# RWKV scan: even heads in one half of the partitions and odd heads in the other, all products 64x64x64

## Chip, core and metric

The kernel runs on one core of one Trainium2 chip. The metric is the device time of one execution in microseconds (us). Three runs of the kernel before gave a median of 3237.41 us (3236.87 to 3237.65).

## What is computed

The program is one transformer block: two modulated layer norms, a token mixer with two branches (neighbourhood attention and an RWKV recurrence), a merge of the branches, and an expert layer. The change touches the recurrence, which runs in both directions (d = 0, 1) over 256 context tokens and then 1024 tokens, for 8 heads of 64:

```
def step(S, inp):
    r_t, w_t, k_t, a_t, v_t, kk_t = inp
    sa = einsum('bhvk,bhk->bhv', S, -kk_t)
    S = S * w_t[:, :, None, :] + sa[..., None] * (kk_t * a_t)[:, :, None, :] + v_t[..., None] * k_t[:, :, None, :]
    y = einsum('bhvk,bhk->bhv', S, r_t)
S, ys = lax.scan(step, S0, xs, reverse=reverse)
```

## The kernel before, in words

The recurrence is computed in chunks of 64 tokens: 20 chunks for each direction, 4 of context and 16 of the sequence. Inside a chunk it is a set of matrix products, so that a chunk and a direction make one step, and one step takes the state S of each head from one chunk's end to the next. The program has these parts in order of time:

- **Projections and features** (the function `mixer`, up to about 898 us of the trace). `proj` multiplies the normalised tokens by the input weights (L256). `feat` makes, for four pairs of heads (`ct` 0 to 3; a pair is two heads of 64 in 128 partitions) and both directions, the operands of every chunk and stores them to DRAM scratch: X (L417), the masked products AQ (L424 to L431), the transposed BK (`BTD`, L439), the token-major values v (`vD`, L361). `inv_load`, `inv` and `inv_off` invert the 64x64 triangles of all chunks on VectorE and store them as `WD`.
- **The scan** (`rwkv_chain`, L513 to L570). A step loads its operands with 7 DMAs on the SP queue, two buffers for each direction: X, AQ in two pieces, BT, WT in two pieces, and v into the lower half of the tile UV. Its products: RY from X and the block-diagonal S (L536, 4 products of 128x128x128) and from AQ and UV (L539, 8 of 128 rows by 64 columns); R = -RY copied by ScalarE and VectorE, one half each (L543, L544); US = WT R (L548, 8 products of 64x64x64); the result copied into the upper half of UV by VectorE and ScalarE (L551); BT UV (L554, 8 products); the state update, an addition and a multiplication for each half (L559, L560, four VectorE instructions); and, after the context, the output's second part (L563, 8 products), a copy on ScalarE (L566) and a store on the ScalarE queue (L567). GpSimd clears the unused quarters of AQ and UV in each step (L527).
- **Attention** (`attention`) runs over four head pairs with 8 blocks each. A block computes scores (L586 to L589), a row maximum with the bias (L590, L591), an exponential on ScalarE (L594), a normalisation (L597), transposes with their copies (L604 to L608), and the output (L611 to L615). The preparation of Q and K of a head pair is in L621 to L641, loads of bias (`bt`, one buffer, L650) and values (`vb`, L655) go out on the ScalarE queue. The pairs 0 and 1 have one PSUM buffer for each kind of tile; the pairs 2 and 3 have two.
- **Readout** (`readout`, L661 to L693) sums both directions' outputs, needs the scan's end, and is followed by modulation chunks (L117) and the two branch products (L707). The expert layer fills the rest from about 1600 us.

A tile framework orders the instructions of each engine when the program is built, by its own estimates and by the order in which the program is written; at run time each engine takes its list in that order. So the place of the attention blocks among the scan's steps is fixed in the program, and can be read from it.

Of the kernel before, what the change touches and what calls it, by code (L numbers as in the profile page):

```python
# [63 lines left out]
def host_layout(i):  # L64

    f=np.float32
# [82 lines left out]
def mixer(octx, tc, i, G, keep, mc, dbg=None):  # L149
# [14 lines left out]
    vnD=dp.tile([TS,512],F32,name="vnD"); vD=dp.tile([TS,512],F32,name="vD")  # L164
    DLD=[dp.tile([4,128,20],F32,name=f"DLD{d}") for d in range(2)]
    XD=[dp.tile([4,128,20,128],F32,name=f"XD{d}") for d in range(2)]
    AQD=[dp.tile([20,128,8,128],F32,name=f"AQD{d}") for d in range(2)]
    BTD=[dp.tile([20,128,4,128],F32,name=f"BTD{d}") for d in range(2)]
    WD=[dp.tile([4,40,64,64],F32,name=f"WD{d}") for d in range(2)]
    aD=[dp.tile([4,2,40,64,32],F32,name=f"aD{d}") for d in range(2)]; sgD=dp.tile([128,T],F32,name="sgD")  # L170
    G.update(dict(XD=XD,AQD=AQD,BTD=BTD,WD=WD,DLD=DLD))
    gD=dp.tile([16,128,T],F32,name="gD")
    yD=[dp.tile([T,512],F32,name=f"yD{d}") for d in range(2)]
# [5 lines left out]
    with ExitStack() as c1:  # L179
# [142 lines left out]
        with ExitStack() as c3:  # L322
# [29 lines left out]
            def on_v(c,ps):  # L352
                ct=(c-2560)//128
                for q,(t0,nt) in enumerate(((0,2),(2,4),(6,4))):
# [6 lines left out]
                    nc.sync.dma_start(vD[t0*128:(t0+nt)*128,ct*128:(ct+1)*128].rearrange("(a p) f -> p a f",p=128),vt[:,:nt])  # L361
# [5 lines left out]
            def feat(ct,mid):  # L367
# [18 lines left out]
                for d in range(2):  # L386
# [21 lines left out]
                    for jb in range(5):  # L408
# [33 lines left out]
                    bo=bonus[:,:,2*ct:2*ct+2]; pv=pt[:,:16].rearrange("p (a b) -> p a b",b=2)  # L442
# [70 lines left out]
def rwkv_chain(p,pR,tc,i,G):  # L513
    nc=tc.nc; vD=G["vD"]; yD=G["yD"]
    S=[p.tile([128,4,2,64],F32,name=f"S{d}",bufs=1) for d in range(2)]
    for d in range(2): nc.gpsimd.memset(S[d],0.0)
    DL=[p.tile([128,4,20],F32,name=f"DLs{d}",bufs=1) for d in range(2)]
    for d in range(2): nc.sync.dma_start(DL[d],G["DLD"][d].rearrange("a p c -> p a c"))
    def step(j,n,d):
        main=j>0; tb=tblock(j,d); c=n if d==0 else 3-n; cc=tb*4+c  # L520
        first=(j==0 and n==0); M=128 if main else 64
        X=p.tile([128,4,128],F32,name=f"cX{d}"); AQ=p.tile([128,8,128],F32,name=f"cAQ{d}")
        BT=p.tile([128,4,128],F32,name=f"cBT{d}"); WT=p.tile([128,4,64],F32,name=f"cWT{d}")
        UV=p.tile([128,512],F32,name=f"UV{d}")
        nc.sync.dma_start(X[:,:,:M],G["XD"][d][:,:,cc,:M].rearrange("a p f -> p a f"))
        nc.sync.dma_start(AQ[64:128,:,:M],G["AQD"][d][cc][64:128,:,:M])
        nc.gpsimd.memset(AQ[0:64,:,0:64],0.0); nc.gpsimd.memset(UV[0:64],0.0)  # L527
        if main: nc.sync.dma_start(AQ[0:64,:,64:128],G["AQD"][d][cc][0:64,:,64:128])
        nc.sync.dma_start(BT,G["BTD"][d][cc])
        for hh in range(2):  # L530
            nc.sync.dma_start(WT[hh*64:hh*64+64],G["WD"][d][:,cc*2+hh,0:64,:].rearrange("a s t -> s a t"))
        nc.sync.dma_start(UV[64:128],vD[cc*64:(cc+1)*64,:])
        RY=pR.tile([128,512],F32,name=f"RY{d}")
        if not first:
            for ct in range(4):
                nc.tensor.matmul(RY[:M,ct*128:(ct+1)*128],X[:,ct,:M],S[d][:,ct].rearrange("p a b -> p (a b)"),  # L536
                    start=(ct==0),stop=False,skip_group_check=True)
        for hd in range(8):
            nc.tensor.matmul(RY[0:64,hd*64:(hd+1)*64],AQ[:,hd,0:64],UV[:,hd*64:(hd+1)*64],  # L539
                start=(first and hd==0),stop=True,skip_group_check=True)  # L540
        R=p.tile([128,4,64],F32,name=f"R{d}",bufs=2)
        ry=RY[0:64].rearrange("p (a b f) -> p a b f",a=4,b=2)
        nc.scalar.activation(R[0:64],ry[:,:,0,:],AF.Copy,scale=-1.0)  # L543
        nc.vector.tensor_scalar_mul(R[64:128],ry[:,:,1,:],-1.0)  # L544
        US=pR.tile([128,512],F32,name=f"US{d}")
        for hd in range(8):
            ct,hh=divmod(hd,2); h=slice(hh*64,hh*64+64)
            nc.tensor.matmul(US[h,ct*64:(ct+1)*64],WT[h,ct,:],R[h,ct,:],start=True,stop=True)  # L548
        uv=UV[0:64].rearrange("p (a b f) -> p a b f",a=4,b=2); us=US[:,0:256].rearrange("p (a f) -> p a f",a=4)
        for hh in range(2):  # L550
            (nc.scalar.copy if hh else nc.vector.tensor_copy)(uv[:,:,hh,:],us[hh*64:hh*64+64])  # L551
        for hd in range(8):
            ct,hh=divmod(hd,2)
            nc.tensor.matmul(US[hh*64:hh*64+64,256+ct*64:256+(ct+1)*64],BT[:,ct,hh*64:hh*64+64],  # L554
                UV[:,hd*64:(hd+1)*64],start=True,stop=True)
        sp=US[:,256:512].rearrange("p (a b) -> p a b",b=64)
        for hh in range(2):
            h=slice(hh*64,hh*64+64); sd=S[d][h,:,hh,:]
            if not first: nc.vector.tensor_add(sd,sd,sp[h])  # L559
            nc.vector.tensor_tensor(sd,sp[h] if first else sd,DL[d][h,:,cc:cc+1].to_broadcast([64,4,64]),op=ALU.mult)  # L560
# [538 lines left out]
```

## Time and profile before

| | us |
|---|---|
| median of three runs | 3237.41 |
| the profiled execution | 3229.26 |
| its span, first to last instruction | 3227.5 |
| TensorE busy, share of the span | 2969.2, 92% |
| VectorE busy | 2357.7, 73% |
| ScalarE busy | 1740.9, 54% |
| GpSimd busy | 640.3, 20% |
| mean granted TensorE clock | 0.958 of full speed |

The profile is of one execution. TensorE's busy time counts a product from its start to its modelled end, so overlapping products make a busy share that is near one long before the array is full. A float32 product shows as two records. Times of day below (898, 1225, ...) are us from the span's start. All further rows stand in the section on rows.

### The profile page before, as it was taken

What the parts mean: (1) busy time and instruction counts of PE and PEld (TensorE: products, weight loads), DVE (VectorE), ACT (ScalarE), POOL (GpSimd) and SP (SyncE); (2) the same over time, 40 slices, a digit from 0 to 9 for tenths busy, and PEclk for the clock granted to TensorE, in tenths of its full rate; (3) what the DMA queues carried; (4) which work ended last, traced back from release to release, by engine and by line L of the source; (5) the groups of instructions that cost most, each with busy time, mean ns of one, the idle gap of its engine ahead of it and who ended that gap; (6) DMA issues with size and microseconds to landing.
All of it is one profiled execution on the core that took longest, in us unless ns stands there. A gap on an engine that the chain in (4) does not pass through costs nothing.

```text
span 3227.5 us, 47411 instructions
## 1 busy us (share of the span) xinstructions
PE 2969.2 (92%) x17900; PEld 2361.8 (73%) x17900; DVE 2357.7 (73%) x3207; ACT 1740.9 (54%) x2006; POOL 640.3 (20%) x511
## 2 busy tenths in 40 slices
PE   5999999998779879999879999999999999999996
PEld 3777777776667765577668888888888878888884
DVE  3335555443566768857779899888888888888887
ACT  4343333333234343432357777777777777777775
POOL 2233333333331326411000000111010111010004
PEclk9999999998789989999889999999999999999998
DMA  5245444455768776544589999999999999999985
GB/s 192 82 125 136 120 117 120 125 139 146 165 175 196 188 184 215 157 158 150 191 317 383 387 372 370 358 360 378 381 362 364 355 365 376 381 362 363 363 319 230
DMA packets 537640, 825.17 MB, mean 256 GB/s; under 512 B 206590, under 2 KB 335742, under 8 KB 537284
## 3 DMA queue, kind: packets, MB, share of 16 engines
q1 hardware_dynamic: 489436, 742.36, 67.3%
q10 hardware_dynamic: 42616, 60.26, 5.9%
q0 software_dynamic: 5360, 19.54, 2.3%
q8 instruction: 141, 2.31, 0.3%
q14 instruction: 87, 0.71, 0.1%
HBM read 732.49 MB, written 89.55 MB: 255 GB/s over the span
## 4 chain that ended last, share of the span: by engine, by line
PE 56%; DVE 14%; DMA 10%; issue 6%; ACT 3%; SPq 2%; POOL 1%; ACTq 0%; POOLq 0%; DVEq 0%
PE ph L1014 21%; PE ye L1029 14%; PE pp L256 7%; DVE lo L913 4%; PE pA L707 3%; PE po L750 2%; DVE tmp L290 1%; DVE W L293 1%; DMA raw<-in_w_e_dram 1%; PE px L424 1%; PE pt L1051 1%; DMA AU<-aD 1%; ACT hi L912 1%; DMA bt<-in_bias_dram 1%; DMA vb<-vnD 1%
## 5 line engine op out<-in xcount | busy, mean ns | idle before, releaser
L913 DVE TENSOR_TENSOR lo<-raw,hi 128x2048 fp32r<-128x2048 f32 (+1 forms) x560 | 1197.4, 2170 | 108.7 <-ACT hi L912 92.6
L912 ACT CAST hi<-raw 128x2048 fp32r<-128x2048 f32 (+1 forms) x560 | 1010.0, 1814 | 355.3 <-PE ph L1014 191.9
L1014 PE MATMUL ph<-lo,xh 128*128 128x512 f32 (+1 forms) x1536 | 456.8, 379 | 23.6 <-DVE lo L913 21.9
L1014 PE MATMUL ph<-hi,xh 128*128 128x512 f32 (+1 forms) x1536 | 449.2, 374 | 3.1 <-ACT xh L884 2.0
L1014 PE MATMUL ph<-hi,xl 128*128 128x512 f32 (+1 forms) x1536 | 448.2, 373 | 0.0
L1014 PEld LDWEIGHTS ph<-lo,xh 128*128 128x128 f32 x1536 | 267.8, 189 | 95.7 <-DVE lo L913 48.4
L1014 PEld LDWEIGHTS ph<-hi,xh 128*128 128x128 f32 x1536 | 271.5, 188 | 55.9 <-ACT xh L884 2.4
L1014 PEld LDWEIGHTS ph<-hi,xl 128*128 128x128 f32 x1536 | 270.9, 188 | 52.5
L256 PE MATMUL pp<-uh,whi 128*128 128x512 f32 (+1 forms) x832 | 263.8, 390 | 4.7 <-DVE th L332 3.1
L256 PE MATMUL pp<-ul,whi 128*128 128x512 f32 (+1 forms) x832 | 266.9, 390 | 0.1
L256 PE MATMUL pp<-uh,wlo 128*128 128x512 f32 (+1 forms) x832 | 261.9, 387 | 1.0 <-issue 0.7
L862 POOL DMA_INDIRECT gath<-table,idx x16 | 37.8, 2364 | 959.2 <-DVE oh L854 587.8
L1029 PE MATMUL ye<-lo,dh 128*128 128x512 f32 x704 | 222.8, 398 | 1.1 <-DVE lo L913 1.1
L1029 PE MATMUL ye<-hi,dh 128*128 128x512 f32 x704 | 219.8, 393 | 2.5 <-ACT hi L912 1.3
L1029 PE MATMUL ye<-hi,dl 128*128 128x512 f32 x704 | 218.9, 392 | 3.1 <-DVE dl L1053 3.1
L256 PEld LDWEIGHTS pp<-uh,wlo 128*128 128x128 f32 x832 | 155.9, 195 | 39.2 <-issue 9.4
L256 PEld LDWEIGHTS pp<-uh,whi 128*128 128x128 f32 x832 | 154.4, 195 | 40.4 <-issue 6.8
L256 PEld LDWEIGHTS pp<-ul,whi 128*128 128x128 f32 x832 | 155.7, 195 | 37.6 <-issue 9.4
L290 DVE TENSOR_TENSOR tmp<-AU,W 120x144 f32<-120x144 f32 (+24 forms) x248 | 88.4, 357 | 116.9 <-DMA WD<-AU 40.8
L1029 PEld LDWEIGHTS ye<-hi,dl 128*128 128x128 f32 x704 | 132.9, 189 | 32.1 <-DVE dl L1053 3.6
L244 POOL TENSOR_TENSOR wlo<-wraw,whi 128x512 fp32r<-128x512 f32 x86 | 113.6, 1339 | 209.4 <-ACT whi L243 141.0
L1029 PEld LDWEIGHTS ye<-hi,dh 128*128 128x128 f32 x704 | 131.2, 189 | 30.7 <-ACT hi L912 2.0
(334 smaller groups left out, 4470.2 us busy)
## 6 DMA issues: line engine op xcount, KB each, us to landing
raw<-in_w_e_dram SPq DMA_DIRECT2D x430, 1024.0 KB
raw<-in_w_e_dram SPq DMA_DIRECT2D x128, 768.0 KB
wraw<-in_w_in_dram SPq DMA_DIRECT2D x86, 256.0 KB
wmod<-in_w_mod_dram SPq DMA_DIRECT2D x48, 256.0 KB
BTD<-BT SPq DMA_DIRECT2D x40, 256.0 KB
cBT<-BTD SPq DMA_DIRECT2D x40, 256.0 KB
wmod<-in_w_mod_dram SPq DMA_DIRECT2D x16, 512.0 KB
XD<-X SPq DMA_DIRECT2D x32, 256.0 KB
```

The lines of the kernel that those rows point to most:

```text
L244: nc.gpsimd.tensor_sub(l[:,ks],r,h[:,ks].bitcast(F32))
L256: nc.tensor.matmul(p,wt[:,k,:],ut[:,k,a:a+b],start=(k==0 and first),stop=(k==7 and last))
L290: nc.vector.tensor_tensor(v,AU[d][:,:,s,ts_][:,:,None,:].to_broadcast([120,2,nj,L]), W[d][:,:,js,s:s+1].to_broadcast([120,2,nj,L]),op=ALU. ...
L293: for o,v in tv: nc.vector.tensor_sub(o,o,v)
L424: for c in range(4): nc.tensor.matmul(pa[:,c,:w],BK[h,c,:],X[h,c,:w],start=True,stop=True)
L707: nc.tensor.matmul(pq[q],w[:,kk,:],y[:,kk,q*512:(q+1)*512],start=(kk==0 and first),stop=(kk==3 and last))
L750: nc.tensor.matmul(pq[q],a[:,r],w[:,q*512:(q+1)*512],start=(k==0 and first),stop=(k==7 and last))
L862: gi=nc.gpsimd.indirect_dma_start(out=g,out_offset=None,in_=table[:,:], in_offset=bass.IndirectOffsetOnAxis(ap=idx[:,:1],axis=0))
L912: nc.scalar.copy(hi[:,:2*w],r[:,:2*w])
L913: li=nc.vector.tensor_sub(lo[:,:2*w],r[:,:2*w],hi[:,:2*w].bitcast(F32))
L1014: nc.tensor.matmul(PH[m][j][:,:c.stop-c.start],x[:,k,:],y[:,c],start=(k==0 and a),stop=(k==7 and b))
L1029: nc.tensor.matmul(ye[j],l[:,k,:],rr[:,j*512:(j+1)*512],start=st and a,stop=sp and b)
```

## The change

Before, an operand of one head could lie in any half of the partitions: AQ held the part for v in partitions 64 to 127 and the part for the corrections in 0 to 63, and both heads of a pair stood side by side in the columns. After the change every operand of an even head lies in partitions 0 to 63 and every operand of an odd head in 64 to 127: AQ becomes AV (for v) and AU (for the corrections U), UV becomes V and U, BT becomes two planes of 64 columns, S loses its zero blocks. Each product of 128 rows becomes two of 64 rows that add up in PSUM, and each is a 64x64x64 product on the diagonal of the array: a step has 64 products where it had 36. The parts that need only loaded data (AV V, BT V) or the old state (X S) stand ahead of the ones that need U. R and U are copied by one ScalarE instruction each over 128 partitions, the state update is two VectorE instructions, the output's copy covers 128 partitions by 256. The clearing by GpSimd is gone. A step has 8 loads (AV, two for V, X, two for WT, BT, AU) and two output stores. The features are stored in this layout: four stores for BTD where there was one, four for AVD and AUD where there were three, two for vD where there was one. The host permutes the columns of g_up, gn and w_pr accordingly.

```
-                        if jb: nc.sync.dma_start(AQD[d][cs,64:128,2*ct:2*ct+2,:]...,AQ[64:128])
                         for hh in range(2):
-                            if jb: nc.sync.dma_start(AQD[d][cs,0:64,2*ct+hh,64:128]...,AQ[0:64,:,hh,64:128])
-                            else: nc.sync.dma_start(AQD[d][cs,64:128,2*ct+hh,:w]...,AQ[64:128,:,hh,:w])
+                            nc.sync.dma_start(AVD[d][cs,hh*64:hh*64+64,ct,:w]...,AQ[64:128,:,hh,:w])
+                            if jb: nc.sync.dma_start(AUD[d][cs,hh*64:hh*64+64,ct]...,AQ[0:64,:,hh,64:128])
...
-                        nc.sync.dma_start(BTD[d][cs,:,ct,:].rearrange("c p f -> p c f"),BT)
+                        for j in range(2):
+                            for hh in range(2):
+                                nc.sync.dma_start(BTD[d][cs,j,hh*64:hh*64+64,ct]...,BT[j*64:j*64+64,:,hh*64:hh*64+64])
...
 def rwkv_chain(p,pR,tc,i,G):
+    H=[slice(0,64),slice(64,128)]
+    def mm(o,l,r,first=None,stop=False):
+        for ct in range(4):
+            for hh,h in enumerate(H):
+                b=first is not None and len(first)<2
+                z=nc.tensor.matmul(o[h,ct],l[h,ct],r[h,ct],start=b,stop=stop,skip_group_check=True)
...
+        nc.sync.dma_start(AV[:,:,:M],G["AVD"][d][cc][:,:,:M])
+        for h,hh in zip(H,range(2)): nc.sync.dma_start(V[h],vD[cc*64:(cc+1)*64,hh])
         nc.sync.dma_start(X[:,:,:M],G["XD"][d][:,:,cc,:M].rearrange("a p f -> p a f"))
...
+        nc.sync.dma_start(BT,G["BTD"][d][cc].rearrange("j p a k -> p j a k"))
+        if main: nc.sync.dma_start(AU,G["AUD"][d][cc])
+        mm(RU[:,0],AV[:,:,0:64],V,[],first)
+        if not first: mm(RU[:,0],X[:,:,0:64],S[d],stop=True)
         R=p.tile([128,4,64],F32,name=f"R{d}",bufs=2)
+        nc.scalar.activation(R,RU[:,0],AF.Copy,scale=-1.0)
+        f=[]
+        mm(YS[:,1],BT[:,1],V,f)
         if main:
+            mm(YS[:,0],AV[:,:,64:128],V,f)
+            mm(YS[:,0],X[:,:,64:128],S[d])
+        mm(RU[:,1],WT,R,stop=True)
+        nc.scalar.copy(U,RU[:,1])
+        mm(YS[:,1],BT[:,0],U,stop=True)
+        if not first: nc.vector.tensor_add(S[d],S[d],YS[:,1])
+        nc.vector.tensor_tensor(S[d],YS[:,1] if first else S[d],DL[d][:,:,cc:cc+1].to_broadcast([128,4,64]),op=ALU.mult)
+        if main:
+            mm(YS[:,0],AU,U,stop=True)
+            Y=p.tile([128,4,64],F32,name="Y",bufs=4)
+            nc.scalar.copy(Y,YS[:,0])
+            for h,hh in zip(H,range(2)): nc.scalar.dma_start(yD[d][(cc-4)*64:(cc-3)*64,hh],Y[h])
```

The order that the framework makes moves with it. On TensorE, in the middle of the scan before, the steps of both directions (RY and US) stand among attention's scores (sc, sl), transposes (apt) and outputs (yp); x8 is eight products of a kind, and the numbers tell tiles apart:

```order
L536 MATMUL RY_8487<-S_7293,cX_8473 128x128 x4
L539 MATMUL RY_8487<-UV_8477,cAQ_8474 64x64 x8
L536 MATMUL RY_8551<-S_7294,cX_8537 128x128 x4
L539 MATMUL RY_8551<-UV_8541,cAQ_8538 64x64 x8
L604 MATMUL apt<-ident,s 128x128
L586 MATMUL sc<-KH_10834,Q_10832 128x256
L587 MATMUL sc<-KL_10836,Q_10832 128x256
L588 MATMUL sl<-KH_10834,Q_10832 128x320
L589 MATMUL sl<-KL_10836,Q_10832 128x320
L548 MATMUL US_8503<-R_8500,cWT_8476 64x64 x8
L548 MATMUL US_8567<-R_8564,cWT_8540 64x64
L611 MATMUL yp<-pT,vc 64x128 x4
```

In the changed program the same engine has, from the first step after the context to the last one, nothing but the scan (all its products have the line of the helper, L533). One step of one direction against the other, in the middle:

```order
L533 MATMUL RU_8850<-R_8868,cWT_8838 64x64 x8
L533 MATMUL RU_8940<-cV_8929,cAV_8926 64x64 x8
L533 MATMUL RU_8940<-S_7460,cX_8925 64x64 x7
L533 MATMUL YS_8851<-U_8840,cBT_8841 64x64 x8
L533 MATMUL RU_8940<-S_7460,cX_8925 64x64
L533 MATMUL YS_8941<-cV_8929,cBT_8931 64x64 x8
L533 MATMUL YS_8941<-cV_8929,cAV_8926 64x64 x7
L533 MATMUL YS_8851<-U_8840,cAU_8837 64x64 x8
L533 MATMUL YS_8941<-cV_8929,cAV_8926 64x64
L533 MATMUL YS_8941<-S_7460,cX_8925 64x64 x8
```

All but one or two of the 16 attention blocks that stood among the scan's steps have moved behind the scan's last step: before, 16 blocks' outputs stand in ScalarE's list between the scan's first and last instruction, and after, none. The 8 blocks of the first head pair now stand among the 8 readouts, then 16 blocks follow with no other work between them, and the last 8 stand among the branch products, as 8 did before.

On ScalarE, a step's copies before stand among attention's casts, copies and loads:

```order
L543 ACTIVATE R_8500<-RY_8487 64x256
L625 DMA qz<-kD 128x512
L543 ACTIVATE R_8564<-RY_8551 64x256
L640 CAST Q_10832<-qz 64x2x128 x2
L640 CAST Q_10833<-qz 64x2x128 x2
L644 DMA vc<-vnD 128x2x128
L606 COPY pT<-apt 120x512
L551 COPY UV_8477<-US_8503 64x4x64
```

After, both directions' copies and stores alternate alone:

```order
L553 ACTIVATE R_10218<-RU_10200 128x256
L567 COPY Y<-YS_10111 128x256
L568 DMA yD_95<-Y 64x256 x2
L560 COPY U_10190<-RU_10200 128x256
L553 ACTIVATE R_10308<-RU_10290 128x256
L567 COPY Y<-YS_10201 128x256
L568 DMA yD_96<-Y 64x256 x2
L560 COPY U_10280<-RU_10290 128x256
```

The exponentials of the first attention block stand ahead of the first R after the context in this list, and those of the second block behind the scan's last U.

## Rows read from the trace of the kernel before

**Rows 1.** Table by stretch: scan, readout with attention, branch products with attention.

```profile
core 0: us, PE busy (x) PEld busy (x) DVE busy (x) ACT busy (x) POOL busy (x), PEclk, DMA share, GB/s
898.00:1225.00 327.00, 267.63 (x3416) 225.86 (x3414) 226.62 (x548) 125.87 (x295) 91.05 (x114) 0.91 0.77 184
1225.00:1350.00 125.00, 111.40 (x595) 55.40 (x595) 110.21 (x241) 55.28 (x123) 80.57 (x61) 0.95 0.67 210
1350.00:1466.00 116.00, 114.99 (x650) 91.71 (x648) 67.71 (x135) 36.57 (x72) 20.49 (x7) 1.00 0.44 139
```

**Rows 2.** One line's instructions: L614 in those three stretches, L566 and L594 over the span.

```profile
L614 ACT CAST yh<-yp x16: 247/265/267, 966.4 to 1198.2; 128x128 fp32r<-128x128 f32 x16
L614 ACT CAST yh<-yp x9: 241/265/273, 1240.0 to 1349.2; 128x128 fp32r<-128x128 f32 x9
L614 ACT CAST yh<-yp x7: 265/265/267, 1359.6 to 1421.0; 128x128 fp32r<-128x128 f32 x7
L566 ACT COPY Y<-RY x32: 580/580/582, 969.9 to 1223.8; 64x512 f32<-64x512 f32 x32
L594 ACT ACTIVATE s<-s,m x64: 758/820/880, 951.3 to 1408.9; 128x576 f32<-128x576 f32 x32, 128x696 f32<-128x696 f32 x32
```

**Rows 3.** Chain of waits in the scan's stretch, two of its longest pieces: start, us, what.

```profile
999.67 8.73 DMA bt<-in_bias_dram
...
1113.51 8.16 DMA vb<-vnD
```

**Rows 4.** Timeline of TensorE, scan products: start, us, engine, line, tiles, form, records.

```profile
1216.91 1.13 PE L536 MATMUL RY<-S,cX 128*128 128x128 f32 x8 [0.98 <-ACT R L543]
1217.97 1.15 PE L539 MATMUL RY<-UV,cAQ 128*64 128x64 f32 x16
...
1067.39 0.68 PE L548 MATMUL US<-R,cWT 64*64 64x64 f32 x16 [1.67 <-DVE R L544]
...
1069.80 1.11 PE L548 MATMUL US<-R,cWT 64*64 64x64 f32 x14
```

**Rows 5.** One line's instructions: loads issued on the SP queue (ns min/median/max).

```profile
L531 SPq DMA_DIRECT2D cWT<-WD x80: 573/593/892, 886.4 to 1207.5; - x80
L532 SPq DMA_DIRECT2D UV<-vD x40: 445/468/707, 846.2 to 1212.5; - x40
L668 SPq DMA_DIRECT2D y<-yD x16: 319/326/437, 1221.6 to 1295.6; - x16
```

**Rows 6.** DMA traffic of 900 to 1220 us in 40 slices: GB/s.

```profile
GB/s 281 211 125 207 117 244 221 165 110 200 192 217 224 205 181 184 211 188 156 233 165 154 259 103 234 189 192 194 200 213 193 169 172 191 225 172 124 204 158 54
```

**Rows 7.** VectorE groups by line and form, 898 to 1466 us: busy us, mean ns | idle before.

```profile
L560 DVE TENSOR_TENSOR S<-S,DLs 64x256 f32<-64x256 f32 x76 | 43.5, 572 | 1.9
L559 DVE TENSOR_TENSOR S<-S,US 64x256 f32<-64x256 f32 x76 | 31.7, 418 | 20.2 <-PE US L554 18.1 <-ACT UV L551 0.5
...
L591 DVE CUSTOM_DVE_ANT_0 s<-sl,bt,m 128x320 f32<-128x320 f32 x32 | 17.5, 548 | 17.9 <-DMA bt<-in_bias_dram 17.2
...
L544 DVE TENSOR_SCALAR R<-RY 64x256 f32<-64x256 f32 x40 | 16.6, 418 | 24.7 <-ACT R L543 23.6
L551 DVE COPY UV<-US 64x256 f32<-64x256 f32 x40 | 16.5, 414 | 13.3 <-PE US L548 11.3 <-issue 1.4
```

**Rows 8.** Features: what the BT copy (L438) waited for, its store, the stretch.

```profile
  DMA BTD<-BT: 12.9, 8
...
L439 SPq DMA_DIRECT2D BTD<-BT x40: 359/562/1249, 191.6 to 827.3; - x40
...
190.00:830.00 640.00, 589.69 (x3859) 461.93 (x3859) 329.62 (x697) 240.19 (x402) 236.49 (x179) 0.93 0.52 131
```

**Rows 9.** Table by stretch, as rows 1: the granted clock is the third value from the end.

```profile
919.00:936.00 17.00, 7.84 (x75) 7.15 (x76) 12.04 (x23) 3.30 (x9) 7.32 (x7) 0.50 0.56 150
950.00:1038.00 88.00, 81.29 (x1081) 67.88 (x1080) 58.46 (x165) 37.46 (x89) 17.51 (x29) 1.00 0.80 191
1069.10:1072.50 3.40, 3.40 (x30) 2.73 (x29) 3.21 (x10) 0.99 (x3) 0.47 (x1) 0.51 0.64 163
```

More of the change, by code (lines that the diff above doesn't have):

```diff
@@ L438, in feat @@
                         nc.scalar.copy(BT,pb.rearrange("p (c f) -> p c f",c=4))
[L439 removed]
+                        for j in range(2):
+                            for hh in range(2):
+                                nc.sync.dma_start(BTD[d][cs,j,hh*64:hh*64+64,ct].rearrange("c p f -> p c f"),BT[j*64:j*64+64,:,hh*64:hh*64+64])
                     pt=px.tile([128,512],F32,name="px")
                     for t in range(8): nc.tensor.matmul(pt[:,2*t:2*t+2],a[:,256+t*128:256+(t+1)*128],hsr[:,ct,2*ct:2*ct+2],start=True,stop=True)
[L442 removed]
+                    bo=bonus.rearrange("p a (h c) -> p a h c",h=2)[:,:,:,ct]; pv=pt[:,:16].rearrange("p (a b) -> p a b",b=2)
                     if d==0: nc.vector.tensor_copy(bo,pv)
@@ L514, in rwkv_chain @@
     nc=tc.nc; vD=G["vD"]; yD=G["yD"]
-    S=[p.tile([128,4,2,64],F32,name=f"S{d}",bufs=1) for d in range(2)]
-    for d in range(2): nc.gpsimd.memset(S[d],0.0)
+    S=[p.tile([128,4,64],F32,name=f"S{d}",bufs=1) for d in range(2)]
     DL=[p.tile([128,4,20],F32,name=f"DLs{d}",bufs=1) for d in range(2)]
     for d in range(2): nc.sync.dma_start(DL[d],G["DLD"][d].rearrange("a p c -> p a c"))
+    H=[slice(0,64),slice(64,128)]
[4 more added lines that the diff above has]
+                z=nc.tensor.matmul(o[h,ct],l[h,ct],r[h,ct],start=b,stop=stop,skip_group_check=True)
+                if b: first.append(z)
+                elif first: tc.add_manual_dep(z.ins,first[hh].ins.name,mybir.DependencyInfo(mybir.DependencyClass.NoSync,mybir.DependencyReason.DATA),reason="order")
     def step(j,n,d):
@@ L528, in step @@
[L528 to L537, printed above, removed]
@@ L538, in step @@
-        for hd in range(8):
-            nc.tensor.matmul(RY[0:64,hd*64:(hd+1)*64],AQ[:,hd,0:64],UV[:,hd*64:(hd+1)*64],
-                start=(first and hd==0),stop=True,skip_group_check=True)
-        R=p.tile([128,4,64],F32,name=f"R{d}",bufs=2)
[L542 to L560, printed above, removed]
-        if main:
-            for hd in range(8):
-                nc.tensor.matmul(RY[64:128,hd*64:(hd+1)*64],AQ[:,hd,64:128],UV[:,hd*64:(hd+1)*64],
-                    start=False,stop=True,skip_group_check=True)
-            Y=p.tile([128,512],F32,name="Y",bufs=2)
-            nc.scalar.copy(Y[64:128],RY[64:128])
-            nc.scalar.dma_start(yD[d][(cc-4)*64:(cc-3)*64,:],Y[64:128])
+        X,AV=[p.tile([128,4,128],F32,name=f"{z}{d}") for z in ("cX","cAV")]
@@ new lines, in step @@
+        AU,WT,V,U=[p.tile([128,4,64],F32,name=f"{z}{d}") for z in ("cAU","cWT","cV","U")]
+        BT=p.tile([128,2,4,64],F32,name=f"cBT{d}")
+        nc.sync.dma_start(AV[:,:,:M],G["AVD"][d][cc][:,:,:M])
+        for h,hh in zip(H,range(2)): nc.sync.dma_start(V[h],vD[cc*64:(cc+1)*64,hh])
+        nc.sync.dma_start(X[:,:,:M],G["XD"][d][:,:,cc,:M].rearrange("a p f -> p a f"))
+        for h,hh in zip(H,range(2)):
+            nc.sync.dma_start(WT[h],G["WD"][d][:,cc*2+hh,0:64,:].rearrange("a s t -> s a t"))
```

35 lines of the change are left out of this document (17 added, 18 removed).

## The prediction

> **What bounds the kernel now.** I read the table by stretch first, from the scan's first product to the last branch product, since nothing after 1466 us changes. Three stages follow one another: the scan with 16 attention blocks (327 us), the readout with 9 blocks (125 us), the branch products with 7 blocks (116 us), together 568 us [rows 1]. The counts are from attention's last cast, one for each block [rows 2]. In the scan no engine is full: TensorE 0.82, VectorE 0.69, DMA 0.77. In the readout VectorE is busy 110 of 125 us, in the branch products TensorE 115 of 116 us [rows 1].
>
> Second, the pace of the scan. The outputs' copies run from 969.9 to 1223.8 us, 32 of them, so 16 pairs of steps (both directions) take 253.9 / 15.5 = 16.4 us each [rows 2]. One attention block goes by in each pair. Third, the chain of waits: its long pieces are loads, of attention's (`bt`, `vb`) as of the scan's own [rows 3]. Each engine takes its list in order, so a block that waits for its bias holds a scan step, and a step that waits holds the block. In return each fills the other's gaps.
>
> The order listing then says what the change is: the scan loses its 16 blocks. Before, a pair and a block shared 16.4 us; now they stand one behind the other. If P is the pair's period alone and b the block's period alone, the whole question is whether P + b is more or less than about 17.
>
> **The scan, part by part.** TensorE: the 128-column products are 8 records in 1.13 us, the last of which ends about 0.28 us after its start, so (1.13 - 0.28) / 7 = 0.12 us a record; L539 is (1.15 - 0.22) / 15 = 0.062; L548, which already is 64x64x64 on the diagonal, is (0.68 - 0.22) / 15 = 0.031, since two of them overlap [rows 4]. A main step before is 8 x 0.12 + 16 x 0.062 twice (L539, L563) + 16 x 0.031 twice (L548, L554) = 3.9 us. After, it is 64 products, 128 records at 0.031: 4.0 us. The array's time does not change; a pair costs TensorE 7.9 us either way. Reading the row so, halving a product's cost is paid back by doubling their number. The Trainium skill (TensorEngine Tiling (Array Packing), section Theoretical Speedup) gives up to 2x for a dimension of at most 64. Applied to every product at an unchanged count, that would bring a pair to about 5 us; L548's row agrees with the 2x for a product, and the count of 64 against 36 is what the rule leaves out.
>
> VectorE: four update instructions (0.42 + 0.57 twice), a copy of R and a copy of U, 2.8 us a step, become two over 128 partitions, 0.42 + 0.42 to 0.57 [rows 7]. Over 40 steps 110 us become about 37. This is real relief, but VectorE waits in the scan anyway. The dependent chain of one direction shrinks from about 6.3 us (two products of 1.1, 0.42, 0.68, 0.42, 0.69, four updates of 2.0) to 0.68 + 0.42 + 0.68 + 0.42 + 0.68 + 0.9 = 3.8 us [rows 4, 7]; both are under half of 16.4 and, with the directions alternating, under P. GpSimd's clearing goes; nobody on the path waited for it for want of GpSimd.
>
> SP queue: 8 issues a step for 7. Two WT at 0.59, two V and X at about 0.47, AV, BT and AU between 0.33 (a full-width load of 2 KB rows) and 0.55: 3.6 to 4.2 us, so 7.2 to 8.4 us a pair [rows 5]. Loads run two steps ahead, so their landing is covered; their rate is not. A step moves 1.31 MB, as before (by the tiles' shapes 256 KB each for AV, X and BT, 128 each for V, WT, AU and the output). At the best slice of the scan now, 281 GB/s, a pair's 2.62 MB take 9.3 us, at the stage's mean of 184 GB/s 14.2 us [rows 1, 6]. So P lies between 7.9 (TensorE) and 14.2. I take 9.4: the rows of TensorE and SP are nearest, and what held the mean rate down was loads queued behind attention, not the engines (DMA 0.77).
>
> Before its main part the scan waits for attention's start: the first block's exponentials stand ahead of the first R after the context in ScalarE's list, and they ended at about 953 us (951.3 and two of 0.82) [rows 2]. I keep that: 55 us from 898, with the context's four pairs inside. Then 16 x 9.4 = 150, and 4 for the last update and output: 209 us against 327.
>
> **Attention alone.** VectorE spends 226.6 us in the scan's stretch, of which the scan has 43.5 + 31.7 + 16.6 + 16.5, so a block with its share of the preparation of Q and K costs at most (226.6 - 108.3) / 16 = 7.4 us [rows 1, 7]. At the share that VectorE reached in its fullest stage, 110 / 125, that is 8.4 us. From above, the seven casts in the branch stage are 61.4 / 6 = 10.2 us apart, with TensorE full [rows 2]. A reason against the lower end: `bt` has one buffer, and its load is issued only behind the row maxima that free it; VectorE already idles 17.2 us for it [rows 7], and a load of it takes up to 8.7 us [rows 3]. With no scan steps to fill this wait it is bare. I take b = 8.8, ends 7.4 and 10.2; 16 x 8.8 = 141 us.
>
> **The rest.** The readout and branch stages keep 16 blocks between them, as before. The first block of the readout stage has its scores and exponentials behind it, about a block's work of 8 us, so 125 - 8 = 117 us; the branch stage stays at 116. In the features four BTD stores stand for one and four AV/AU for three: 40 x 3 + 32 + 12 for vD = 164 issues of about 0.56 us, 92 us of the SP queue over 640 us. The copy that waits for this store waited 12.9 us in all, 8 times; three more issues before each of 40 buffers come free, 1.7 us, are 67 us at most, on a ScalarE that is busy 240 of 640 us [rows 8]. TensorE's projections cover it (0.92 busy): 0, and up to 10 if that cover has holes.
>
> **Sum.** 55 + 150 + 4 + 117 + 141 + 116 = 583 us for 568: 15 us more. Against the profiled execution, 3229.3, that is 3244; the median of the runs shown is 8 us above it, 3237.4, so 3252. In general the change is 16 (P + b) - 276: the limit is P + b = 17.25.
>
> **Rivals.** *Faster*: in the shared stage each engine's list was held by the other's loads [rows 3]; apart, both run at their own engine's pace. P = 8.0 (TensorE and SP) and b = 7.6 (VectorE, nearly full) give 16 x 15.6 - 276 = -26 us, 3211. For it: the main part's lists alternate without a foreign instruction. Against it: the single `bt` buffer. It decides where b is under 7.8 at my P.
>
> *Loads do not come faster*: the scan's own bytes are the same. If the 184 GB/s were what this mix can do, P = 14.2 and the change is +92 us, 3329. Against it: slices of 281, 259 and 244 GB/s [rows 6].
>
> *The clock falls*: a step that waits for loads leaves TensorE idle, and in 919 to 936 us, when it was busy 7.8 of 17 us, it had 0.50 of its clock, 1.2 GHz; at 1.00 it was busy 81 of 88 us [rows 9]. At 0.51, the same product took (1.11 - 0.37) / 13 = 0.057 us a record [rows 4, 9], so a pair would take 256 x 0.057 = 14.6 us: +98 us, 3335; if only the lone attention blocks are slowed, to 10.2, +37, 3275. Against it in the scan: at P = 9.4 TensorE has work for 7.9 us. The Trainium skill (TensorE: Matmul & The Clock Gate, section HAM oscillation) tells of short groups of products between DMA waits that start cold each time. By that rule the time is the 3335 above; the rows at 0.50 agree with it for sparse work, and no row here shows diagonal products alone for long.
>
> **Chances.** Forecast 0.50: P between 8.6 and 10.5 and b between 8.2 and 10.2. Faster 0.33, loads slow 0.08, clock 0.09. About 0.2% (6.5 us) is what a measurement of this kernel can tell from no change. Of the forecast's part 0.13 lies within that, and the rest above: faster 0.33, same 0.13, slower 0.54. The range for 8 in 10 goes from 3206 (P 7.9, b 7.4, 31 us saved) to 3299 (P 10.9, b 10.2, 62 us lost), and leaves out the two slowest cases. The likeliest case's own range is 3230 to 3292.
>
> **What would show it.** The scan's last update at about 1107 us instead of 1225; the output copies 9.4 us apart for each direction; no attention cast before that end; then 16 casts without readout or branch products, 8.8 us apart, with VectorE idle for `bt` before the row maximum of L591 (L592 in the new code); branch products ending about 1481. I am wrong if the copies are over 11 us apart (loads, or the clock row at 0.5), or if the 16 lone blocks come at 7.6 us or less.

## The result, and the profile after

The changed kernel takes 3328.7 us (median; 3322.6 to 3332.7) beside 3237.1 us for the kernel before (3233.7 to 3237.7): 1.0277 times as long, 95% interval 1.0256 to 1.0298, about 92 us slower. Forecast were 3252 and a range that ended at 3299: the change was slower, as forecast, but by far more. The profiled execution's span is 3320.8 us, 93 us over the one before.

The table by stretch, as [rows 1]: start of the scan, its main part, readout with 8 blocks, 16 lone blocks, a pause, branch products with 8 blocks.

```profile
core 0: us, PE busy (x) PEld busy (x) DVE busy (x) ACT busy (x) POOL busy (x), PEclk, DMA share, GB/s
911.00:975.00 64.00, 43.95 (x767) 38.84 (x768) 28.33 (x60) 19.61 (x45) 23.34 (x18) 0.71 0.68 189
975.00:1157.00 182.00, 137.67 (x4020) 132.70 (x4015) 30.32 (x72) 36.33 (x97) 1.36 (x2) 0.92 0.75 211
1157.00:1267.00 110.00, 90.07 (x458) 41.99 (x456) 87.86 (x173) 43.30 (x98) 72.09 (x52) 0.91 0.65 204
1267.00:1425.00 158.00, 115.60 (x692) 73.72 (x692) 100.64 (x284) 66.22 (x161) 35.69 (x33) 0.75 0.24 72
1425.00:1434.00 9.00, 5.57 (x17) 4.14 (x17) 6.51 (x24) 5.17 (x15) 1.13 (x1) 0.50 0.62 179
1434.00:1558.00 124.00, 122.34 (x696) 97.50 (x696) 75.33 (x152) 38.97 (x79) 20.47 (x7) 0.98 0.42 132
```

The stages are those that the prediction named, and no block ends before the scan does. Their sum is 647 us where 583 were forecast and 568 stood before; the scan also begins 12.7 us later, at 911.1 for 898.4 us. VectorE's relief came (30 of 182 us busy) and paid nothing. The single lines that answer to [rows 2, 4, 8], with the last 13 of the lone blocks' casts:

```profile
L567 ACT COPY Y<-YS x32: 372/372/373, 977.3 to 1156.3; 128x256 f32<-128x256 f32 x32
...
L615 ACT CAST yh<-yp x13: 244/266/267, 1316.0 to 1424.9; 128x128 fp32r<-128x128 f32 x13
...
L533 PE MATMUL RU<-cV,cAV x640: 213/218/311, 911.1 to 1147.3; 64*64 64x64 f32 x160
...
L446 SPq DMA_DIRECT2D BTD<-BT x160: 574/615/2065, 191.9 to 846.8; - x160
...
  DMA BTD<-BT: 56.1, 21
```

The outputs' copies (L567) give the pair: (1156.3 - 977.3) / 15.5 = 11.55 us, forecast 9.4. The casts give (1424.9 - 1316.0) / 12 = 9.08 us for a block that really is alone, forecast 8.8; over all 16 it is 158 / 16 = 9.9, since the first of them took 25 us beside the readout's end. The last row is what BT's copy in the features waited for: 56.1 us where [rows 8] had 12.9.

Inside the scan of the change, the waits of 980 to 1150 us (engine line <- released by: us, times, longest), and behind them the timeline of one:

```profile
PE YS L533 <- ACT U L560: 43.2, 26, 4.2
ACT U L560 <- DMA yD<-Y: 39.5, 12, 5.2
```

```profile
1061.67 1.38 ACTq L568 DMA_DIRECT2D yD<-Y  x2
...
1062.75 1.44 SPq L548 DMA_DIRECT2D cAU<-AUD  x1
1063.10 0.37 ACT L560 COPY U<-RU 128x256 f32<-128x256 f32 x1 [2.37 <-DMA cV<-vD]
1063.52 0.68 PE L533 MATMUL YS<-U,cBT 64*64 64x64 f32 x16 [1.35 <-ACT U L560]
```

U's copy stands in ScalarE's list behind the other direction's two output stores, whose issue took 1.38 us, and TensorE waits for U. SP meanwhile is hardly ever idle.

From this came the first theory (the stores on ScalarE make the pair 11.55), with the loads as rival; the runs made it three questions: what sets the lone pair, what the features cost, and what the lost sharing costs.

### The profile page after: what moved, and what is told of

Same layout as the page of the kernel before. It is cut to its first block, busy times and chain, and to the rows that moved or that the text cites. A ratio compares the mean times of both kernels' runs of the same rounds, so it can differ in the third digit from the quotient of the medians.

```text
span 3320.8 us, 51369 instructions
## 1 busy us (share of the span) xinstructions
PE 3000.9 (90%) x19868; PEld 2380.2 (72%) x19868; DVE 2287.1 (69%) x3049; ACT 1738.2 (52%) x2008; POOL 596.7 (18%) x429
## 4 chain that ended last, share of the span: by engine, by line
PE 56%; DVE 17%; DMA 13%; issue 5%; SPq 4%; ACT 4%; POOL 1%; ACTq 1%; POOLq 0%; DVEq 0%
PE ph L1016 21%; PE ye L1031 13%; PE pp L261 7%; DVE lo L915 4%; PE pA L709 2%; PE po L752 2%; DVE tmp L295 2%; DVE W L298 2%; DMA raw<-in_w_e_dram 2%; PE YS L533 2%; SPq L446 1%; DMA cV<-vD 1%; DMA AU<-aD 1%; PE px L430 1%; PE pt L1053 1%
## 5 line engine op out<-in xcount | busy, mean ns | idle before, releaser
L295 DVE TENSOR_TENSOR tmp<-AU,W 120x144 f32<-120x144 f32 (+24 forms) x248 | 99.5, 401 | 103.8 <-DMA AU<-aD 30.9
```

The lines of the kernel that those rows point to most:

```text
L295: nc.vector.tensor_tensor(v,AU[d][:,:,s,ts_][:,:,None,:].to_broadcast([120,2,nj,L]), W[d][:,:,js,s:s+1].to_broadcast([120,2,nj,L]),op=ALU. ...
```

## The experiments

All times are us. An issue is the instruction that starts a DMA, in the list of the engine that starts it. "Pair" is from the outputs' copies (last minus first, over 15.5), "first" is the scan's first product; ratios are to the kernel before, run beside each.

| run | whole | ratio, 95% interval | pair | first |
|---|---|---|---|---|
| the change | 3328.7 | 1.0277, 1.0256 to 1.0298 | 11.55 | 911.1 |
| e1 U on VectorE | 3349.7 | 1.0364, 1.0346 to 1.0381 | 11.95 | 912.6 |
| e2 stores on GpSimd | 3314.7 | 1.0251, 1.0233 to 1.0268 | 10.54 | 914.2 |
| e3 BT in two stores | 3341.4 | 1.0338, 1.0321 to 1.0355 | 12.71 | 908.5 |
| e4 blocks back | 3315.0 | 1.0256, 1.0238 to 1.0273 | 20.33 with a block | 916.1 |
| e5 = e2, WT on GpSimd | 3315.8 | 1.0237, 1.0220 to 1.0254 | 10.47 | 913.6 |
| e6 = e2, fewer bytes | 3312.1 | 1.0227, 1.0210 to 1.0244 | 10.77 | 909.2 |
| e7 one tile | 3344.7 | 1.0321, 1.0304 to 1.0338 | 10.09 | 959.7 |
| e8 bias once | 3318.2 | 1.0251, 1.0232 to 1.0270 | 11.75 | 918.8 |
| e9 BT's stores on ScalarE | 3346.2 | 1.0338, 1.0321 to 1.0355 | 11.80 | 935.8 |
| e10 = e5 and e6 | 3281.1 | 1.0139, 1.0122 to 1.0157 | 9.15 | 911.3 |
| e11 = e4 and e2 | 3306.0 | 1.0215, 1.0198 to 1.0233 | 19.05 with a block | 914.6 |
| e12 dense order | 3277.2 | 1.0124, 1.0107 to 1.0141 | mixed | 915.2 |
| e13 old layout, apart | 3339.2 | 1.0326, 1.0307 to 1.0344 | 11.53 | 907.4 |
| e14 dense, BT in two | 3262.9 | 1.0089, 1.0071 to 1.0107 | mixed | 907.3 |
| e15 dense from the start | 3256.3 | 1.0067, 1.0047 to 1.0086 | mixed | 911.9 |
| e16 = e14, fewer issues | 3252.5 | 1.0051, 1.0034 to 1.0068 | mixed | 904.7 |
| e17 = e16, V on GpSimd | 3259.4 | 1.0071, 1.0050 to 1.0093 | mixed | 901.5 |
| e18 = e16, blocks first | 3262.7 | 1.0085, 1.0065 to 1.0104 | mixed | 906.8 |

### What sets the lone pair

**e1.**

```
-        nc.scalar.copy(U,RU[:,1])
+        nc.vector.tensor_copy(U,RU[:,1])
```

> Only U's copy out of PSUM moves from ScalarE to VectorE. Theory (ScalarE's list): in the changed kernel a pair of scan steps takes 11.55 us and not 9.4 because U's copy stands behind two output stores on ScalarE (TensorE idles 111 us before the scan's products for U). Then the pair falls to 9.4 to 10.2 and the scan's main part from 182 to 150 to 160 us; the whole to 3297 to 3308. Rival (the loads): the pair needs 2.62 MB and the DMA engines give 211 GB/s in this mix; then the pair stays at 11.2 to 11.6 and the whole at 3322 to 3330. Rival (the clock, 0.92 in this part): no change of the pair beyond 0.3 us either.

The pair did not fall. The wait had moved to the next copy in ScalarE's list, R's (waits of e1, 960 to 1130 us):

```profile
ACT R L553 <- DMA yD<-Y: 90.3, 17, 6.3
...
PE RU L533 <- ACT R L553: 46.8, 25, 4.7
```

The whole is 21 us worse. The edit moved the order of the program too: the first block's cast comes 49 us after the scan's last output (1187.8), for 3.5 us in the change. So this run decides nothing on the stores; e2 does.

**e2.**

```
-            ...: nc.scalar.dma_start(yD[d][(cc-4)*64:(cc-3)*64,hh],Y[h])
+            ...: nc.gpsimd.dma_start(yD[d][(cc-4)*64:(cc-3)*64,hh],Y[h])
```

> Only the scan's output stores move from ScalarE's queue to GpSimd's, which has nothing to do in the scan. Theory (ScalarE's list): the same cause taken away from the other side, and R's and Y's copies no longer stand behind stores either: pair 9.0 to 9.8, whole 3290 to 3305, at least as much as with U's copy on VectorE. Rival (the loads): pair 11.2 to 11.6, whole 3322 to 3330.

1.0 us a pair of the 2.15 came back: the stores on ScalarE's queue were a real cost, but not the floor. What SP does then (timeline of e2, SP alone):

```profile
1050.02 0.56 SPq L547 DMA_DIRECT2D cBT<-BTD  x1
1050.67 0.42 SPq L548 DMA_DIRECT2D cAU<-AUD  x1
1051.18 0.38 SPq L542 DMA_DIRECT2D cAV<-AVD  x1
1051.62 1.16 SPq L543 DMA_DIRECT2D cV<-vD  x2
1052.87 0.53 SPq L544 DMA_DIRECT2D cX<-XD  x1
1053.50 2.42 SPq L546 DMA_DIRECT2D cWT<-WD  x2
1056.02 0.56 SPq L547 DMA_DIRECT2D cBT<-BTD  x1
```

From BT to BT is one step, 6.0 us (the mean is 5.3), and SP issues with hardly a pause (0.1 us at most between the rows). The new theory: 8 issues a step set the pace, not the bytes.

**e6 and e5.** One takes bytes away and leaves the issues (heads 4 to 7 are computed with the operands of heads 0 to 3), the other the reverse; **e10** does both. All three have e2's stores.

```
 e6, e10: -  nc.sync.dma_start(AV[:,:,:M],G["AVD"][d][cc][:,:,:M])
          +  nc.sync.dma_start(AV[:,:,:M],G["AVD"][d][cc][:,0:2,:M])    (BT, AU alike)
 e5, e10: -  nc.sync.dma_start(WT[h],G["WD"]...)
          +  nc.gpsimd.dma_start(WT[h],G["WD"]...)
```

> As the run with the output stores on GpSimd's queue, but the loads of AV, BT and AU bring only the first half of their columns (heads 4 to 7 are computed with the operands of heads 0 to 3), so a step loads 0.86 MB for 1.18, by the same number of issues and products. Theory (the number of SP's issues sets the pace): pair 9.8 to 10.5 (a little under 10.54, as fewer issues are held back), whole 3303 to 3315. Rival (the DMA engines set it): bytes fall by 27%, so the pair falls to TensorE's 8.5 to 9.0 and the whole to 3281 to 3292.

> As the run with the output stores on GpSimd's queue (pair 10.54 us, whole 3314.7), and the two loads of WT of each step go there too: SP issues 6 loads a step, not 8, and the bytes stay. Theory (the scan alone runs at the pace of SP's issues: 8 of them at 0.4 to 0.8 us and 0.05 between them are 5.3 us a step, and SP is never idle): SP needs about 7.6 us a pair, so TensorE (8.5 us a pair at full clock) or the loads are next: pair 8.6 to 9.6, whole 3284 to 3302. Rival (the DMA engines set the pace, 237 GB/s, and SP's issues are long because of it): pair 10.2 to 10.7, whole 3308 to 3318.

> Both of the earlier edits together: output stores and WT's loads on GpSimd's queue (SP issues 6 loads a step) and half the columns of AV, BT and AU (0.86 MB a step). Issues alone left the pair at 10.47 us, bytes alone at 10.77. Theory (two limits stand side by side at about 10.5 us, SP's issues and the bytes at 240 to 256 GB/s, and behind both stands TensorE at 8.5): pair 8.5 to 9.2, whole 3280 to 3296. Rival (a third thing holds the pair, such as the dependent chain of one direction's step): 10.2 to 10.8, whole 3305 to 3316.

Tables by stretch of e6, e5 and e10 (columns as above):

```profile
985.00:1130.00 145.00, 111.91 (x3310) 106.27 (x3307) 21.99 (x52) 29.31 (x78) 27.43 (x52) 0.98 0.64 175
```

```profile
985.00:1130.00 145.00, 113.43 (x3536) 110.30 (x3538) 26.17 (x58) 31.19 (x83) 67.91 (x112) 0.96 0.89 241
```

```profile
985.00:1100.00 115.00, 99.84 (x3224) 96.80 (x3225) 21.22 (x51) 28.19 (x75) 56.26 (x97) 1.00 0.79 211
```

With 27% fewer bytes the pair stays at 10.77 and the DMA engines fall to 0.64: bytes alone do not hold it. With 6 issues SP idles (in e5 the load of AU, L548, alone waits 34.0 of 145 us for TensorE's products), and the pair still stays at 10.47, now with the DMA engines at 0.89. Only both together free it: 9.15, TensorE at full clock and busy 0.87. GpSimd issues as much in e10 as in e5, so it is not what held e5. So two limits stood side by side near 10.5 us, SP's issues and the bytes, and neither edit alone shows its worth; TensorE's own share of it is 99.84 / 115 x 9.15 = 7.9.

**e3 and e7** change the number of issues in the features too.

```
 e3: -  for j in range(2): for hh in range(2): nc.sync.dma_start(BTD[d][cs,j,hh*64:...,ct],BT[j*64:...,hh*64:...])
     +  for hh in range(2): nc.sync.dma_start(BTD[d][cs,hh,:,ct],BT[:,:,hh*64:hh*64+64])
     -  nc.sync.dma_start(BT,G["BTD"][d][cc]...)
     +  for h,hh in zip(H,range(2)): nc.sync.dma_start(BT[h],G["BTD"][d][cc,hh]...)
 e7: +  A=p.tile([128,4,320],...); nc.sync.dma_start(A[:,:,:MA],G["AQD"][d][cc][:,:,:MA])
     +  nc.sync.dma_start(WT,G["WD"][d][cc*2:cc*2+2]...); nc.sync.dma_start(V,vD[cc]...); nc.scalar.dma_start(yD[d][cc-4]...,Y)
```

> The features' store of BT becomes two issues instead of four (a buffer with the halves outermost; the scan then loads BT in two pieces, one issue more a step). Theory (SP's queue sets the end of the features: its issues of 0.6 us and the store before BT's buffer comes free stand on the chain from 815 to 840 us): the scan's first product comes 4 to 9 us earlier than 911.1, at 902 to 907, and the whole falls by 3 to 9 us if the ninth issue of a step costs the scan nothing. Rival (the features are late for their bytes or for TensorE): first product at 910 to 912, whole 3328 or more.

> Same halves, same products, but AV, BT and AU lie in one buffer (5 KB a partition), V, WT and the output have both halves outermost per chunk: SP issues 4 loads a step instead of 8, ScalarE one store instead of two, for the same bytes. The features issue more stores (AV in two pieces, V in four). Theory (the issues set the pace): SP needs under 6 us a pair, so TensorE's 8.5 us is the bound and the pair takes 8.6 to 9.2; main part 135 to 145 us for 182; whole 3280 to 3298, the features' stores costing 2 to 8 us more. Rival (the DMA engines at 211 to 237 GB/s): pair 10.3 to 11.5, whole 3312 to 3335.

A ninth issue in each step costs the lone pair 1.16 us; four issues on SP for eight, and one on ScalarE for two, bring it to 10.09, at 252 GB/s. That is near the second limit, the bytes, but no run took bytes away from e7. And e7's 88 further stores in the features, of smaller pieces, put the scan 46 us back. The Trainium skill (SBUF — State Buffer, section The DMA setup-cost knee) advises coalescing into few large transfers because of a fixed cost in each. e7's scan agrees in direction (10.09 us for 11.55), and its features show the price of the other side: BT's copy waited 83.8 us for its stores, in the change 56.1. In the lone scan e2 and e6 show the cost of an issue as time in the list of the engine that issues it.

### What the features cost

**e9.**

```
-    nc.sync.dma_start(BTD[d][cs,j,...],BT[...])
+    nc.scalar.dma_start(BTD[d][cs,j,...],BT[...])
```

> The changed kernel with the four stores of BT in the features on ScalarE's queue, right behind the copy that fills their buffer; the scan is untouched. Theory (SP's list of stores is what delays the features: BT's copy waited 56.1 us for its own stores, 12.9 us in the kernel before): the first product of the scan comes at 896 to 904 us for 911 to 919 in the runs with the changed features so far, and the whole falls by 8 to 14 us, to 3315 to 3321. Rival (the stores cost as much wherever they stand, since ScalarE now issues 160 of them, 90 us): 908 to 918, whole 3324 to 3332.

Against the theory, the scan starts 25 us later still. Of the lines on the tile BT in e9, the first says that its copy now waits little for its stores; but ScalarE spends the issues itself, and the next copy on it, AQ's, stands behind them (54.6 us, in the change 3.3):

```profile
  DMA BTD<-BT: 3.0, 4
...
  ACT AQ L431: 54.6, 21
```

So 160 issues of 0.6 us delay whatever list they stand in. In the ten profiles with the changed features the first product comes at 909 to 919 us, mean 913.7; with BT in two stores (six profiles, three of them with WT's buffer ordered anew as well) at 901 to 912, mean 906.8; with the old ones (two) at 898.4 and 907.4. The features' cost is thus some 11 us between the means, though the two old profiles lie 9 us apart. Two stores fewer return 7 of it by all six runs, and 4 to 5 by the three that keep WT's buffer (e3, e14, e15, mean 909.2).

### What the lost sharing costs

**e8.** The lone blocks by themselves:

```
-    if ii!=2:  bt=...; q_(bt[:,:,:N],i["bias"][ii,hc,...])
+    if ii==0 and hc==0:  bt=...; q_(bt,i["bias"][1,hc,...])
```

> The changed kernel, but attention loads its bias once for each pair of heads instead of six times (the other blocks take that first bias), so no row maximum waits for it. Theory (the bias in its one buffer holds the lone blocks; it is 12.7% of the chain there, and holds ScalarE's exponentials and VectorE by turns): the 16 lone blocks take 8.4 to 9.2 us instead of 9.86, whole 3308 to 3322. Rival (the preparation of Q and K with the dependent steps at half clock sets them): 9.6 to 10.0, whole 3323 to 3331.

The same 13 casts as above, in e8:

```profile
L615 ACT CAST yh<-yp x13: 251/266/267, 1318.3 to 1418.5; 128x128 fp32r<-128x128 f32 x13
```

(1418.5 - 1318.3) / 12 = 8.35 us for 9.08: the single bias buffer is worth 0.7 us a block, the wait that the prediction said would stand bare, and 8 (by the ratios) to 10 us in all, with intervals that overlap.

**e4, e11, e12** put the blocks back by their priority alone: one behind each pair (e4; with e2's stores, e11), or, in e12, which has e2's stores too, none for 13 outputs and then two a pair.

```
+    low_priority(tc,-3000) around att((0,1),...); tc.cur_priority+=100 behind each of its blocks   (e12: -2000, no step)
```

> Only the order changes: attention's first 16 blocks are given priorities that put one block behind each pair of the scan's steps, as in the kernel before. Theory (what was lost is the sharing: apart, a pair and a block take 11.55 + 9.86 = 21.4 us, together they took 16.4): the 64 + 182 + 158 us of start-up, scan and lone blocks become 327 us or less and the 9 us of pause before the branch products go, but the readout stage gets its 125 us back: whole 3235 to 3260. Rival (the stores in ScalarE's list hold a shared pair as they hold a lone one, and a block's two transfers of bias and values come on top): pair with block 18 to 20 us, whole 3270 to 3310. Rival (sharing is worth nothing): 3325 to 3335.

> One attention block behind each pair, as in the run with the blocks back (20.33 us for pair and block, whole 3315.0), and the output stores on GpSimd's queue. Theory (the stores in ScalarE's list hold the shared pair too): 18.5 to 19.5 us, whole 3285 to 3303. Rival (TensorE, 16.7 us busy of 20.3 at a clock of 0.86, with its own list of 256 products of the scan a pair between a block's dependent products): 19.9 to 20.6, whole 3307 to 3320.

> As the run before it, with the order alone changed: the first 13 outputs of the scan come alone, then one block for each output, two for a pair, over the second half. Theory (what the sharing is worth hangs on the order): the first 6 pairs at 10.5 us, then 9 pairs with 16 blocks at 27 to 30 us each, where separate they would take 10.5 + 2 x 9.1 = 28.7; whole 3285 to 3305. Rival (any sharing costs as much as none, TensorE's list being the bound): 30 us or more a pair with two blocks, whole 3308 to 3325.

Evenly spread, pair and block take 20.33 us, hardly less than 11.55 + 9.08 apart, and far from the 16.4 before. TensorE is busy 247 of 300 us at a clock of 0.86, before 207 of 245 at 0.93, that is 16.7 us for a pair and its block where it was 13.9 (tables by stretch of e4, and of the kernel before):

```profile
990.00:1290.00 300.00, 246.86 (x4358) 199.46 (x4356) 125.88 (x317) 95.07 (x239) 28.10 (x21) 0.86 0.54 149
```

```profile
970.00:1215.00 245.00, 206.99 (x2654) 173.61 (x2651) 169.49 (x419) 100.08 (x236) 55.63 (x77) 0.93 0.80 189
```

The stores' place is worth 1.3 us of it (e11). Order alone, from e11 to e12, is worth 29 us: what sharing gives hangs on how the two lists are woven. e2 and e12 too differ in the order alone: with the blocks apart 3314.7, with e12's weave 3277.2, so that sharing is worth 38 us in the new layout (41 by the ratios). Why the even weave is the worse was not settled.

**e13** turns the question round: the old layout in the new order.

```
     def q_(*a):          # attention's loads, ordered behind the scan's last output store
+        z=nc.scalar.dma_start(*a); tc.add_manual_dep(z.ins,G["ly"].ins.name,...)
```

> The kernel before, layout and instructions as they were, but attention's loads are ordered behind the scan's last output store, so its first 16 blocks run after the scan as in the changed kernel. Theory (the order is the cause: the old layout alone is bound by the same bytes, 10 to 11 us a pair): pair 10.2 to 11.2, then blocks at 9.1 us as in the changed kernel; whole 3295 to 3315, that is 60 to 78 of the 92 us without any new layout, the rest being the features' 12.7 us and SP's issues. Rival (the layout is the cause): the old pair alone takes 9 us or less with its 7 loads and half as many products, whole under 3285. Rival (the new layout is better and only the order spoils it): pair over 12, whole over 3325.

Its outputs' copies, and the table by stretch of its scan and of what follows up to the last branch product:

```profile
L566 ACT COPY Y<-RY x32: 580/580/581, 951.6 to 1130.3; 64x512 f32<-64x512 f32 x32
```

```profile
965.00:1130.00 165.00, 130.93 (x2054) 119.73 (x2053) 72.16 (x173) 37.70 (x85) 25.59 (x52) 0.94 0.97 216
1130.00:1582.00 452.00, 358.92 (x1909) 232.06 (x1907) 286.21 (x690) 169.10 (x377) 149.44 (x110) 0.81 0.39 122
```

The old scan alone takes 11.53 us a pair too, and the whole is 3339.2: with not one operand moved, an order with the blocks apart costs 108 us (its kernel before took 3231.1). By the rows the equal pair does not have the same limit: here SP stands still for 43 of 165 us and the DMA engines are 0.97 busy at 216 GB/s, in the change SP stands still for 17 of 170 us and the DMA engines are 0.75 busy at 211. The old layout's scan has far more small packets for the same bytes (first e13, 965 to 1130 us; then the change, 980 to 1150 us):

```profile
DMA packets 52559, 35.65 MB, mean 216 GB/s; under 512 B 30341, under 2 KB 43653, under 8 KB 52535
```

```profile
DMA packets 53637, 36.85 MB, mean 217 GB/s; under 512 B 18270, under 2 KB 50019, under 8 KB 53603
```

One reserve: e13's order is not quite the changed kernel's, since attention's preparation also begins only behind the scan, and its first cast comes 86 us after it. Behind the scan e13 takes 452 us where the change takes 401; its scan, with no attention in its start, takes 223 us for 245. So by these stretches some 29 to 51 of the 108 us are the later preparation (an estimate) and the rest the order asked about. For the same reason the 10 us by which e13 is slower than the change do not tell which layout is better in one order.

**e14 to e18** look for the best the new layout can do. (In e16 to e18, as in e7, the readout loads each direction's output in two pieces.)

```
 e14, e15: e2 and e3 with low_priority(tc,-2300) or (tc,-3000) around att((0,1),...)
 e16: e14 at -2600, WT in one load, the output in one store on GpSimd's queue;  e17: V's loads on GpSimd's too;  e18: e16 at -3500
```

> New layout, output stores on GpSimd, BT stored in two pieces by the features, order: ten outputs alone, then two blocks for a pair. Theory (in a shared stretch SP has time for a ninth load, and the features' gain of some 5 us is kept): 3265 to 3275 for 3277 with four pieces. Rival (the ninth load costs as it did in the lone scan): 3277 to 3295.

> As the run before, with the blocks from the scan's first outputs on, two for a pair, and the second half of the scan alone. Theory (only how many blocks run beside a pair counts): within 6 us of the run before. Rival (blocks late are better, as the lone pairs then run while the loads of Q and K come, and the readout finds the scan's last outputs): 3280 to 3305.

> New layout, BT stored in two pieces, WT in one load (its buffer ordered by chunk, half and row), the output in one store on GpSimd's queue: 8 loads and 1 store a step for 9 and 2; six outputs of the scan alone, then two blocks a pair, then the last pairs alone. Theory (SP's issues hold the lone pairs of this order as they held the lone scan): lone pairs 10.3 us or less for 11 to 12, whole 3243 to 3256. Rival (the lone pairs are few and the shared stretch has its own bound in TensorE): 3256 to 3266, as the run with the blocks from the start.

> As the run before, with the values' two loads on GpSimd's queue: SP issues 6 loads a step. Theory (SP's issues): another 2 to 8 us, 3238 to 3252; rival (the bytes at 240 to 256 GB/s are reached): no change beyond 4 us from the run before.

> As the first of these three, with a block behind each output from the start and the second half of the scan alone. Theory (only how many blocks run beside a pair counts, not when): within 6 us of it. Rival (late blocks are better, since the loads of Q and K are then behind the scan's start): 8 to 20 us slower.

e14 is 14 us faster than e12 in spite of its ninth load, but its order differs too, so the load's price in a shared stretch stays open. e16 has the lowest time, 3252.5 us: 76 us of the 92 are back, 15 are not, and no run comes under the kernel before; e15's interval overlaps e16's. Fewer issues on SP than e16's brought nothing (e17). With the blocks early instead of late e15 takes 7 us less than e14 and e18 takes 10 us more than e16, each with intervals that overlap, so no side is shown for their place. The lines of e16's first product and outputs:

```profile
L532 PE MATMUL RU<-cV,cAV x640: 217/219/367, 904.7 to 1224.8; 64*64 64x64 f32 x160
...
L565 ACT COPY Y<-YS x32: 347/372/374, 964.1 to 1230.8; 128x256 f32<-128x256 f32 x32
```

In e16, scan and 16 blocks take 904.7 to 1230.8, 326 us, as before (327 in [rows 1]). What it still loses lies around them: the scan starts 6 us later (898.4 before), and from its last output to the end of the branch products, 1488.9 us, pass 258 us, where 242 stood before.

## Why the prediction was wrong

**Right:** that everything turns on P + b against 17.25; that the scan runs alone first, that then the blocks run alone; that TensorE's time for a pair hardly falls (7.9 us forecast; busy 7.9 in e10, 8.5 in e2 and 8.7 in the change, beside 9.1 for the old layout alone in e13); that VectorE's relief pays nothing; the readout and branch stages (110 + 124 us for 117 + 116, with 8 blocks each); the lone block (9.1 us for 8.8).

**The step that failed: "I take 9.4"** for P. It measured 11.55, that is 28 us over the main part's 154. The prediction took the best slice, 281 GB/s, and SP at 7.2 to 8.4 us a pair, and it put ScalarE's list at nothing, without a reason. Three sizes were off, each shown by a run: the two stores on ScalarE's queue 1.0 us (e2), SP's 8 issues 10.5 to 10.8 and not 8.4 (e6), the loads 10.1 to 10.5 at 241 to 252 GB/s and not 9.3 (e5, e7). For SP the sum took issues at the length of single rows, 3.6 to 4.2 us a step; in the step of e2 shown above 8 of them take 6.0 us with their pauses, long ones among them. With all three eased the pair is 9.15 (e10). Its ground for the best slice, that loads queued behind attention and not the engines held the mean rate, fails in e13: alone, the old mix moves 216 GB/s with the DMA engines 0.97 busy. The rival *Loads do not come faster* named 3329, nearly the time measured, but that is chance: its P was 14.2 and the pair's is 11.55, the rest of the loss lies in other stages, and with 27% fewer bytes alone the pair did not move. Bytes are one of two limits, and at 241 GB/s, not 184. Nor did *The clock falls*: 0.92 in the main part. It fell where blocks stand alone (0.75), which is inside the 9.9.

**Features "0, and up to 10":** 12.7 us between the two profiles, some 11 between the means. "TensorE's projections cover it" failed: the bound of 67 us was the right kind of term, the cover had holes.

**Smaller terms:** the start-up took 64 us for 55 at a clock of 0.71; the lone blocks 158 for 141, most of it in the one that ran beside the readout's end; a pause of 9 us before the branch products, in which attention's last head pair is prepared, was not foreseen. Together: 15 forecast + 28 + 12.7 + 9 + 17 + 9 + 8 (branch) - 7 (readout) = 92.

## What to carry to other kernels

When a change makes one stage light, look first at what the scheduler had woven into it: here the weave alone was worth 38 us (e2 to e12), more than any edit of the scan that left its work whole, and the old layout lost 108 us with its blocks put behind the scan, a part of them by the later preparation. Price each DMA by its issue on the engine that issues it, at the length that the trace shows when issues follow each other without a pause, and name what stands behind it in that list. Where two limits lie close together, take both away at once before calling either harmless.

## What the runs showed of the hardware

In the lone scan about one issue in each step takes 1.0 to 2.2 us instead of 0.4 to 0.6, on SP whichever load it is. The table of DMA queues (packets, MB, share of the engines) shows about one instruction transfer of 16 KB for a step there (the change, 980 to 1150 us, 29 steps; behind it the kernel before, 970 to 1215 us, 30 steps with their blocks):

```profile
q8 instruction: 30, 0.49, 1.3%
```

```profile
q8 instruction: 22, 0.36, 0.6%
```

By the start times of these transfers, 26 of the 27 SP loads over 0.9 us in the change's main part (975 to 1157 us) have one that begins within the issue or half a us around it, 27 of 28 in e2's and 29 of 29 in e6's; of the shorter issues about 2 in 10 do. A step now has 128 records of products and as many weight loads, before 72; that the longer instruction stream holds SP's issues was not tried by itself. A transfer alone does not make a long issue: in e5, where SP has 6 loads a step and pauses, as many transfers come (31 in its main part), but 8 issues are over 0.9 us. In e6, with its DMA engines at 0.64, the long issues stayed, so full DMA engines are not needed for them. The cause stays open.
